# A hybrid HGRN2 and ConvFFN layer on one core: weights moved to byte 64 of their 256-byte lines, and products of 512 columns divided into two of 256

## The chip, the core and the metric

The kernel runs on one core of a Trainium2 chip. The core has a matrix engine (TensorE; its products stand in the profile as PE, its loads of the stationary operand as PEld), a vector engine (VectorE, DVE), a scalar engine (ScalarE, ACT), GpSimd (POOL) and a queue engine (SyncE, SP) that issues the transfers here. The metric is the device time of one execution in microseconds (us), as the median of several runs; lower is better.

## The reference

One layer of a diffusion backbone over 256 latent tokens and 256 context tokens of width 2048, in float32. It is cut here to what matters.

```python
h_l = modulate(rms_norm(x_lat, norm_mix_pre), sh_ml, sc_ml)      # shifts, scales, gates: silu(c) @ ada_w + ada_b
h_c = modulate(rms_norm(x_ctx, norm_mix_pre), sh_mc, sc_mc)
y_l, _ = hgrn2_mixer(h_l, h_c, w_in, lower_bounds, o_norm, w_out, False)   # w_in 2048 x 10240: q, f, b, v, g
x_lat = x_lat + gt_ml * rms_norm(y_l, norm_mix_post)             # w_out 2048 x 2048
h_l = modulate(rms_norm(x_lat, norm_ffn_pre), sh_fl, sc_fl)
gate, up = split(h_l @ ffn_w_in)                                 # 2048 x 11264
f_l = (silu(dwconv3(gate) ) * up) @ ffn_w_out                    # 5632 x 2048
return x_lat + gt_fl * rms_norm(f_l, norm_ffn_post)
```

The mixer is a gated linear recurrence in both directions over 16 heads of 128, in chunks. Its context half only makes the start state.

## The kernel before

**Products in three parts.** Every weight and every activation of the large products is split into two numbers in the format float32r: `split` (L95, L96) has ScalarE write the rounded `hi` and VectorE the rest `lo`. One product is then three of the matrix engine, in `mm3`: `hi*hi` (L192), `hi*lo` (L193) and `lo*hi` (L194), summed in one bank of PSUM. Each of the three loads its own stationary operand of 128 columns, also where it is the one loaded before.

**The weight stream.** `Stream` walks through 456 weight tiles of 512 KB each (128 partitions x 1024 numbers): 160 of `w_in`, 32 of `w_out`, 176 of `ffn_w_in`, 88 of `ffn_w_out`. Each is loaded into `w_raw` (4 buffers, line L117, queue SP), split by ScalarE into `w_hi` and by VectorE into `w_lo` (3 buffers each), and then used by the matrix engine. [...]

**Where operands lie.** The function `shifted` makes a buffer 32 numbers wider than the tile and puts tile number i of the stream 16*(i mod 8) bytes behind the buffer's start. A buffer is thus 4224 bytes wide, 16.5 times 256. In the built program the three `w_hi` buffers start at bytes 39424, 43648 and 47872 of each partition and the three `w_lo` buffers at 52096, 56320 and 60544: by their remainder to 256 at 0, 128, 0 and at 128, 0, 128. Together with the shift, a tile's `hi` lies at one of the 16 multiples of 16 below 256, and its `lo` always 128 away from it (modulo 256). The other operands have fixed remainders: the normed tokens of the mixer (`hTh`, `hTl`) and the FFN's inner activations (`ah`, `al`) 224, the mixer's output (`zh`, `zl`) 160, the tokens of the FFN's first product (`h2h`, `h2l`) 0. Slices of all these start whole multiples of 512 bytes further. Below, the offset of a product is the start of the stationary operand minus that of the moving one, modulo 256.

**Two directions, two widths.** In one direction weights are stationary and tokens move (the profile writes `pj<-hTh,w_hi`, moving operand first): 256 columns for q, g and for all of `ffn_w_in`, 512 columns for the f and b parts of `w_in` (latent and context tokens at once). In the other direction tokens are stationary and weights move (`pj<-w_hi,hTh`): 256 columns for v after the first two head pairs, 512 columns for v of these, for `w_out` (`pj<-w_hi,zh`) and for `ffn_w_out` (`pj<-w_hi,ah`).

**The order.** Five stages follow one another: the start (norms, the first parts of the modulation by `ada_w`, and four heads, all K at once), the other heads with the recurrence of earlier ones between the products (`scan`), the product with `w_out`, the FFN's first product, its second. Between them VectorE computes the other parts of the modulation from `ada_w` (`ada_part`, L344 and L346, tiles of 256 KB by the same queue SP, 3 buffers). A scheduler that knows shapes orders each engine's instructions within these bounds.

Of the kernel before, what the change touches and what calls it, by code (L numbers as in the profile page):

```python
# [8 lines left out]
F32 = mybir.dt.float32  # L9
F32R = mybir.dt.float32r  # L10
# [7 lines left out]
P = 128  # L18
# [17 lines left out]
def tile_hgrn2_convffn_layer(  # L36
# [17 lines left out]
    ps_mi = ctx.enter_context(tc.tile_pool(name="ps_mi", bufs=1, space=PSUM))  # L54
    ps_o = ctx.enter_context(tc.tile_pool(name="ps_o", bufs=1, space=PSUM))

    def bank(pool, name):
        return pool.tile([P, 512], F32, name=name)

# [35 lines left out]
        S.copy(out=hi, in_=src)  # L95
        V.tensor_tensor(out=lo, in0=src, in1=hi.bitcast(F32), op=ALU.subtract)  # L96

    def shifted(pool, a, w, name, i):

        t = pool.tile([P, a * w + 32], F32R, name=name)  # L100
        return t[:, 4 * i:4 * i + a * w].rearrange("p (a n) -> p a n", a=a)

    class Stream:


# [14 lines left out]
        def prep(self, pool=wpool):  # L120
            i = len(self.done)
            with tc.high_priority(offset=0 if i < n_start else 400):
                self.load(i + 1)
                _, a, w = self.specs[i]
                hi = shifted(pool, a, w, "w_hi", i % 8)
                lo = shifted(pool, a, w, "w_lo", i % 8)
                if i in self.fine:
                    for j in range(a):
                        split(hi[:, j], lo[:, j], self.raw[i][:, j])
                else:  # L130
                    split(hi, lo, self.raw[i])
            self.raw[i] = None
            self.done.append((hi, lo))
# [55 lines left out]

    def mm3(o, lhs, rhs, first, last):  # L190
        (lh, ll), (rh, rl) = lhs, rhs
        PE.matmul(out=o, lhsT=lh, rhs=rh, start=first, stop=False, skip_group_check=True)  # L192
        PE.matmul(out=o, lhsT=lh, rhs=rl, start=False, stop=False, skip_group_check=True)  # L193
        PE.matmul(out=o, lhsT=ll, rhs=rh, start=False, stop=last, skip_group_check=True)  # L194
# [311 lines left out]
    with tc.manual_schedule():  # L506
# [3 lines left out]
        nc.sync.dma_start(out=rowsB[0:96], in_=rows128(ada_b))  # L510
        nc.sync.dma_start(out=rows0[0:16], in_=rows128(n_mix_pre[0]))
        ws.load(1)
        aws0 = ada_load(0)
        ws.load(4)
        V.memset(ones32, 1.0)
# [386 lines left out]
    yp = y_ctx.enter_context(tc.tile_pool(name="yp", bufs=1, side="right"))  # L902
    zh = [yp.tile([P, 2, T], F32R, name=f"zh{p}") for p in range(NP)]
    zl = [yp.tile([P, 2, T], F32R, name=f"zl{p}") for p in range(NP)]
    h_ctx, xin_ctx = ExitStack(), ExitStack()
    h2h, h2l, xin, hold = [], [], [], []

    def mixed():

        nonlocal h2  # L910
        with tc.high_priority(offset=200):
            split(zh[1], zl[1], z[1])
        for p in (*range(2, NP - 1), 0):
            split(zh[p], zl[p], z[p])
            for _ in range(MIXSTEP):
                next(mix, None)
            yield
        for _ in mix:
            pass
        split(zh[NP - 1], zl[NP - 1], z[NP - 1])  # L920
        yield
        yield
        zp_ctx.close()
        sp_ctx.close()
        h2 = h_ctx.enter_context(tc.tile_pool(name="h2", bufs=1))
        for k in range(KT // 2):
            h2h.append(h2.tile([P, 2, T], F32R, name=f"h2h{k}"))
            h2l.append(h2.tile([P, 2, T], F32R, name=f"h2l{k}"))

        xinp = xin_ctx.enter_context(tc.tile_pool(name="xinp", bufs=1))  # L930
        hold.append(xin_ctx.enter_context(tc.tile_pool(name="hold", bufs=MORE)))
        for i in range(4):
            xin.append(xinp.tile([P, D // 2], F32, name=f"xin{i}"))
            nc.sync.dma_start(out=xin[i], in_=x[i // 2 * P:(i // 2 + 1) * P, i % 2 * 1024:(i % 2 + 1) * 1024])

    h2 = None
# [91 lines left out]
    for i in range(NFF):  # L1028
# [6 lines left out]
        for up in range(2):  # L1035
            o = bank(ps_pj, "pj")
# [72 lines left out]
```

## Time and profile before

| | us |
|---|---|
| median of 3 runs | 1764.19 (1764.08 to 1764.83) |
| the profiled execution | 1765.91 |
| its span | 1764.1 |
| matrix engine busy | 1718.5 (97%) |
| VectorE, ScalarE busy | 1158.9, 778.1 |
| mean granted clock of the matrix engine | 0.993 of full speed |

The profiled execution is 1.8 us longer than its span, and 1.7 us longer than the median. A matmul's busy time in the profile is its stay in the pipeline and overlaps with the next one's; how fast products follow one another is read from their starts, or from the number of products in a stretch that is busy throughout.

### The profile page before, as it was taken

The page shows a single profiled execution, that of the slowest core. Times are in us where ns is not written, and L with a number is a line of the kernel's source. Part 1 is how long each engine was busy: PE and PEld are TensorE (multiplying, and loading weights), DVE is VectorE, ACT ScalarE, POOL GpSimd, SP SyncE. Part 2 cuts the span into 40 slices and gives each one's busy share as a digit, 9 for nine tenths or more (in the row PEclk, how much of TensorE's full clock was granted, in tenths as well). Part 3 has the DMA queues.
Part 4 walks back from the last instruction along what each step waited for, and adds up shares of the span by engine and source line. Part 5 has one row for each costly group of instructions (what it writes and reads, how often), then busy time and mean ns, then how long its engine had stood idle before and what let it go on. Part 6 is the DMA issues. An engine that isn't in the chain of part 4 may idle for free.

```text
span 1764.1 us, 32106 instructions
## 1 busy us (share of the span) xinstructions
PE 1718.5 (97%) x13022; PEld 1530.1 (87%) x13022; DVE 1158.9 (66%) x1877; ACT 778.1 (44%) x1197; POOL 3.4 (0%) x13
## 2 busy tenths in 40 slices
PE   6999999999999999999999899999999999999998
PEld 4777788989889888988987699999999999888886
DVE  6777898855649775784667887565555565544444
ACT  4222264444545344443554644444444444443443
POOL 0000000000000000000000000000000000000000
PEclk9999999999999999999999899999999999999999
DMA  9887656643337764774368587566566565655554
GB/s 347 291 306 229 210 167 216 218 141 108 97 96 221 259 204 142 252 227 135 111 235 286 172 290 247 182 190 183 183 185 188 183 191 182 201 196 192 196 188 147
DMA packets 274646, 352.57 MB, mean 200 GB/s; under 512 B 12954, under 2 KB 197675, under 8 KB 273987
## 3 DMA queue, kind: packets, MB, share of 16 engines
q1 hardware_dynamic: 274499, 350.53, 61.6%
q8 instruction: 102, 1.67, 0.4%
q14 instruction: 45, 0.37, 0.1%
HBM read 348.37 MB, written 2.11 MB: 199 GB/s over the span
## 4 chain that ended last, share of the span: by engine, by line
PE 76%; DMA 11%; DVE 8%; issue 2%; ACT 2%; SPq 0%; DVEq 0%; ACTq 0%
PE pj L192 24%; PE pj L194 23%; PE pj L193 23%; DMA ada_w<-in_ada_w_dram 10%; DVE ada_acc L346 3%; DVE w_lo L96 2%; PE o L398 2%; PE sc L713 1%; ACT w_hi L95 1%; PE mi L785 1%; DMA aw<-in_ada_w_dram 0%; DVE k L673 0%; DMA w_raw<-in_hgrn_w_in_dram 0%; PE mi L701 0%; PE o L804 0%
## 5 line engine op out<-in xcount | busy, mean ns | idle before, releaser
L96 DVE TENSOR_TENSOR w_lo<-w_raw,w_hi 128x1024 fp32r<-128x1024 f32 (+1 forms) x465 | 558.5, 1203 | 383.8 <-ACT w_hi L95 382.6
L95 ACT CAST w_hi<-w_raw 128x1024 fp32r<-128x1024 f32 (+1 forms) x465 | 478.6, 1032 | 728.7 <-PE pj L193 395.7
L194 PE MATMUL pj<-h2h,w_lo 128*128 128x256 f32 x1408 | 395.9, 281 | 2.5 <-DVE w_lo L96 2.5
L193 PE MATMUL pj<-h2l,w_hi 128*128 128x256 f32 x1408 | 396.4, 282 | 0.1
L192 PE MATMUL pj<-h2h,w_hi 128*128 128x256 f32 x1408 | 396.0, 281 | 0.2 <-ACT h2h L95 0.2
L192 PE MATMUL pj<-hTh,w_hi 128*128 128x256 f32 (+1 forms) x1040 | 354.0, 341 | 2.8 <-ACT hTh L95 1.6
L194 PE MATMUL pj<-hTh,w_lo 128*128 128x256 f32 (+1 forms) x1040 | 347.9, 335 | 2.9 <-DVE w_lo L96 2.8
L193 PE MATMUL pj<-hTl,w_hi 128*128 128x256 f32 (+1 forms) x1040 | 348.0, 335 | 0.0
L194 PEld LDWEIGHTS pj<-h2h,w_lo 128*128 128x128 f32 x1408 | 265.8, 189 | 3.1 <-DVE w_lo L96 3.0
L192 PEld LDWEIGHTS pj<-h2h,w_hi 128*128 128x128 f32 x1408 | 265.7, 189 | 1.2 <-issue 0.8
L193 PEld LDWEIGHTS pj<-h2l,w_hi 128*128 128x128 f32 x1408 | 265.7, 189 | 0.3 <-DVE h2l L96 0.3
L346 DVE SCALAR_TENSOR_TENSOR ada_acc<-ada_w,cst,ada_acc 128x512 f32<-128x512 f32 x240 | 179.8, 749 | 77.9 <-DMA ada_w<-in_ada_w_dram 75.5
L192 PEld LDWEIGHTS pj<-hTh,w_hi 128*128 128x128 f32 x1040 | 195.5, 188 | 32.3 <-issue 5.9
L194 PEld LDWEIGHTS pj<-hTh,w_lo 128*128 128x128 f32 x1040 | 195.5, 188 | 25.7 <-DVE w_lo L96 3.5
L193 PEld LDWEIGHTS pj<-hTl,w_hi 128*128 128x128 f32 x1040 | 196.0, 188 | 21.0 <-DVE hTl L96 0.2
L192 PE MATMUL pj<-w_hi,ah 128*128 128x512 f32 x352 | 138.8, 394 | 0.0
L194 PE MATMUL pj<-w_hi,al 128*128 128x512 f32 x352 | 138.5, 393 | 0.0
L193 PE MATMUL pj<-w_lo,ah 128*128 128x512 f32 x352 | 138.1, 392 | 0.0
L192 PE MATMUL pj<-w_hi,hTh 128*128 128x256 f32 (+1 forms) x448 | 135.9, 303 | 1.3 <-DVE stage L448 0.7
L194 PE MATMUL pj<-w_hi,hTl 128*128 128x256 f32 (+1 forms) x448 | 133.8, 299 | 0.0
L193 PE MATMUL pj<-w_lo,hTh 128*128 128x256 f32 (+1 forms) x448 | 133.5, 298 | 0.0
L192 PEld LDWEIGHTS pj<-w_hi,hTh 128*128 128x128 f32 x448 | 85.0, 190 | 6.2 <-DVE stage L448 1.8
(224 smaller groups left out, 1778.8 us busy)
## 6 DMA issues: line engine op xcount, KB each, us to landing
w_raw<-in_ffn_w_in_dram SPq DMA_DIRECT2D x176, 512.0 KB, 4.5
w_raw<-in_hgrn_w_in_dram SPq DMA_DIRECT2D x160, 512.0 KB, 4.3
ada_w<-in_ada_w_dram SPq DMA_DIRECT2D x256, 256.0 KB, 3.9
w_raw<-in_ffn_w_out_dram SPq DMA_DIRECT2D x88, 512.0 KB, 3.7
aw<-in_ada_w_dram SPq DMA_DIRECT2D x64, 512.0 KB, 8.0
w_raw<-in_hgrn_w_out_dram SPq DMA_DIRECT2D x32, 512.0 KB, 5.6
hTh<-in_x_dram SPq DMA_DIRECT2D x2, 1024.0 KB, 7.1
hTh<-in_ctx_dram SPq DMA_DIRECT2D x2, 1024.0 KB, 11.8
```

Source lines behind the costliest of these rows:

```text
L95: S.copy(out=hi, in_=src)
L96: V.tensor_tensor(out=lo, in0=src, in1=hi.bitcast(F32), op=ALU.subtract)
L192: PE.matmul(out=o, lhsT=lh, rhs=rh, start=first, stop=False, skip_group_check=True)
L193: PE.matmul(out=o, lhsT=lh, rhs=rl, start=False, stop=False, skip_group_check=True)
L194: PE.matmul(out=o, lhsT=ll, rhs=rh, start=False, stop=last, skip_group_check=True)
L346: V.scalar_tensor_tensor(out=acc, in0=aw, scalar=cst[:, r, 0:1], in1=acc, op0=ALU.mult, op1=ALU.add)
L398: PE.matmul(out=strip[32 * a:32 * (a + 1), :], lhsT=cst[:, r4 * 4 + a, :], rhs=aws[r4][:, a].rearrange("p s n -> p (s n)"), start=(r4 == 0 ...
L713: PE.matmul(out=o[32 * b:32 * b + 32, 32 * i:32 * i + 32], lhsT=flat(lhs[b % 2])[:, s0:s0 + 32], rhs=flat(rhs[b % 2])[:, t0:t0 + 32], star ...
L785: PE.matmul(out=sps[:, cs], lhsT=kT[:, d, h, ct], rhs=v[:, 2 + ct, h * P:(h + 1) * P], start=(ct == 0), stop=(ct == 1))
```

## The change

Three things change. The buffers `w_hi` and `w_lo` lose the shift and are 4096 bytes wide; small unused tiles (`spacer`) are put into the pools so that every weight buffer starts 64 bytes behind a multiple of 256, and `hTh`, `hTl`, `h2h`, `h2l`, `zh`, `zl`, `ah` and `al` on a multiple of 256. In the built program this holds for all products but 24, those with the first split of head pair 0 (`z0`), where both operands are at 64. `hi` and `lo` of a tile thus have the same offset: 64 where weights are stationary, and minus 64, that is 192, where tokens are. And `mm3` divides a product of 512 moving columns into two of 256, each with its three parts.

```diff
+    def spacer(pool, nbytes):
+        pool.tile([P, nbytes // 4], F32, name="spacer", bufs=1)
+    SHIFT = 64
+    edge = ctx.enter_context(tc.tile_pool(name="edge", bufs=1, side="right"))
+    spacer(edge, 224)
...
-    def shifted(pool, a, w, name, i):
-        t = pool.tile([P, a * w + 32], F32R, name=name)
-        return t[:, 4 * i:4 * i + a * w].rearrange("p (a n) -> p a n", a=a)
...
-                hi = shifted(pool, a, w, "w_hi", i % 8)
-                lo = shifted(pool, a, w, "w_lo", i % 8)
+                hi = pool.tile([P, a, w], F32R, name="w_hi")
+                lo = pool.tile([P, a, w], F32R, name="w_lo")
...
     def mm3(o, lhs, rhs, first, last):
         (lh, ll), (rh, rl) = lhs, rhs
+        if rh.shape[-1] == 512:
+            for s in (slice(0, 256), slice(256, 512)):
+                mm3(o[:, s], lhs, (rh[:, s], rl[:, s]), first and s.start == 0, last and s.start > 0)
+            return
         PE.matmul(out=o, lhsT=lh, rhs=rh, start=first, stop=False, skip_group_check=True)
         PE.matmul(out=o, lhsT=lh, rhs=rl, start=False, stop=False, skip_group_check=True)
         PE.matmul(out=o, lhsT=ll, rhs=rh, start=False, stop=last, skip_group_check=True)
...
         ws.load(1)
+        spacer(wpool, SHIFT)
...
+    spacer(yp, 192)
...
         h2 = h_ctx.enter_context(tc.tile_pool(name="h2", bufs=1))
+        spacer(h2, 256 - SHIFT)
...
         hold.append(xin_ctx.enter_context(tc.tile_pool(name="hold", bufs=MORE)))
+        spacer(hold[0], SHIFT)
```

The built program grows from 11694 to 14814 products on the matrix engine: 3120 of 512 columns become 6240 of 256, each with a load of its stationary operand. 1488 of the 3120 (496 in each of the three parts) have stationary weights, 1632 stationary tokens.

On the matrix engine, where the FFN's second product begins, before (line, operation, output, moving and stationary operand with the tile's number, columns):

```order
L194 MATMUL pj<-h2h_10178,w_lo 128x256
L192 MATMUL pj<-w_hi,ah_10796 128x512
L193 MATMUL pj<-w_lo,ah_10796 128x512
L194 MATMUL pj<-w_hi,al_10797 128x512
L192 MATMUL pj<-w_hi,ah_10796 128x512
L193 MATMUL pj<-w_lo,ah_10796 128x512
L194 MATMUL pj<-w_hi,al_10797 128x512
```

And the same place after the change (lines are 10 further):

```order
L204 MATMUL pj<-h2h_11961,w_lo 128x256
L202 MATMUL pj<-w_hi,ah_12868 128x256
L203 MATMUL pj<-w_lo,ah_12868 128x256
L204 MATMUL pj<-w_hi,al_12869 128x256
L202 MATMUL pj<-w_hi,ah_12868 128x256
L203 MATMUL pj<-w_lo,ah_12868 128x256
L204 MATMUL pj<-w_hi,al_12869 128x256
L202 MATMUL pj<-w_hi,ah_12868 128x256
L203 MATMUL pj<-w_lo,ah_12868 128x256
L204 MATMUL pj<-w_hi,al_12869 128x256
L202 MATMUL pj<-w_hi,ah_12868 128x256
L203 MATMUL pj<-w_lo,ah_12868 128x256
```

Each group of three stands there twice, for the two halves of the columns.

On SP's queue, where the weights of the FFN's first product begin, before (`w_raw` is a weight tile, `ada_w` a tile of the modulation's last part):

```order
L117 DMA w_raw<-in_hgrn_w_out_dram 128x2x512
L342 DMA ada_w<-in_ada_w_dram 128x512
L117 DMA w_raw<-in_ffn_w_in_dram 128x4x256 x4
L342 DMA ada_w<-in_ada_w_dram 128x512 x3
L117 DMA w_raw<-in_ffn_w_in_dram 128x4x256 x3
L342 DMA ada_w<-in_ada_w_dram 128x512 x6
L117 DMA w_raw<-in_ffn_w_in_dram 128x4x256
L342 DMA ada_w<-in_ada_w_dram 128x512
```

And after the change:

```order
L122 DMA w_raw<-in_hgrn_w_out_dram 128x2x512
L352 DMA ada_w<-in_ada_w_dram 128x512
L122 DMA w_raw<-in_ffn_w_in_dram 128x4x256 x4
L352 DMA ada_w<-in_ada_w_dram 128x512 x4
L122 DMA w_raw<-in_ffn_w_in_dram 128x4x256 x3
L352 DMA ada_w<-in_ada_w_dram 128x512 x9
L122 DMA w_raw<-in_ffn_w_in_dram 128x4x256
L352 DMA ada_w<-in_ada_w_dram 128x512
```

Four more tiles of `ada_w` stand ahead of the ninth weight tile of the FFN. The loads, their number and their sizes are the same over the whole program; in the stage of the recurrence, too, some instructions of VectorE, ScalarE and SP stand a few places earlier or later than before.

## Rows read from the trace of the kernel before

**Rows 1.** The page: span, busy time by engine (share of the span, instructions).

```profile
span 1764.1 us, 32106 instructions
...
PE 1718.5 (97%) x13022; PEld 1530.1 (87%) x13022; DVE 1158.9 (66%) x1877; ACT 778.1 (44%) x1197; POOL 3.4 (0%) x13
```

**Rows 2.** Windows by stage: busy us (instructions), granted clock, DMA share, GB/s.

```profile
0.00:100.00 100.00, 82.41 (x554) 61.96 (x555) 67.43 (x142) 39.93 (x60) 1.38 (x9) 1.00 0.92 320
100.00:255.00 155.00, 155.00 (x859) 122.39 (x858) 125.71 (x226) 54.04 (x66) 0.00 (x0) 1.00 0.68 225
255.00:890.00 635.00, 627.89 (x5845) 561.34 (x5844) 443.74 (x887) 294.38 (x571) 0.99 (x2) 0.99 0.55 174
...
1005.00:1512.00 507.00, 504.21 (x4245) 502.46 (x4244) 322.17 (x382) 235.39 (x281) 0.53 (x1) 1.00 0.65 200
1512.00:1764.00 252.00, 244.74 (x1061) 198.47 (x1059) 118.07 (x109) 96.42 (x105) 0.00 (x0) 0.99 0.56 186
```

**Rows 3.** Groups by line and shape: count, busy us, mean ns of one.

```profile
L192 PE MATMUL pj<-h2h,w_hi 128*128 128x256 f32 x1408 | 396.0, 281 | 0.2 <-ACT h2h L95 0.2
...
L192 PE MATMUL pj<-hTh,w_hi 128*128 128x512 f32 x496 | 198.7, 401 | 0.0
...
L192 PE MATMUL pj<-hTh,w_hi 128*128 128x256 f32 x544 | 155.3, 287 | 2.8 <-ACT hTh L95 1.6 <-ACT w_hi L95 1.3
...
L192 PE MATMUL pj<-w_hi,ah 128*128 128x512 f32 x352 | 138.8, 394 | 0.0
...
L192 PE MATMUL pj<-w_hi,hTh 128*128 128x256 f32 x384 | 110.4, 287 | 0.0
```

**Rows 4.** Windows, matrix engine alone, inside the FFN's two products.

```profile
1250.00:1500.00 250.00, 250.00 (x2118) 1.00 0.61 186
1520.00:1740.00 220.00, 220.00 (x953) 1.00 0.58 193
```

**Rows 5.** Timeline, FFN's first product: first matmuls of weight tiles 51 to 54.

```profile
1156.79 0.28 PE L192 MATMUL pj<-h2h,w_hi 128*128 128x256 f32 x1
...
1159.63 0.28 PE L192 MATMUL pj<-h2h,w_hi 128*128 128x256 f32 x1
...
1162.36 0.28 PE L192 MATMUL pj<-h2h,w_hi 128*128 128x256 f32 x1
...
1165.19 0.28 PE L192 MATMUL pj<-h2h,w_hi 128*128 128x256 f32 x1
```

**Rows 6.** Timeline, the same product: first matmuls of tiles 60 and 61.

```profile
1182.27 0.28 PE L192 MATMUL pj<-h2h,w_hi 128*128 128x256 f32 x1
...
1185.13 0.28 PE L192 MATMUL pj<-h2h,w_hi 128*128 128x256 f32 x1
```

**Rows 7.** Timeline, mixer, 256 columns, stationary weights: one tile's first matmul, the next's.

```profile
733.31 0.28 PE L192 MATMUL pj<-hTh,w_hi 128*128 128x256 f32 x1
...
736.04 0.28 PE L192 MATMUL pj<-hTh,w_hi 128*128 128x256 f32 x1
```

**Rows 8.** Timeline, 512 columns, stationary weights: one tile's first matmul, the next's.

```profile
130.62 0.39 PE L192 MATMUL pj<-hTh,w_hi 128*128 128x512 f32 x1
...
136.19 0.40 PE L192 MATMUL pj<-hTh,w_hi 128*128 128x512 f32 x1
```

**Rows 9.** Timeline, 256 columns, stationary tokens: second and 47th matmul of one tile.

```profile
437.85 0.28 PE L193 MATMUL pj<-w_lo,hTh 128*128 128x256 f32 x1
...
443.16 0.28 PE L193 MATMUL pj<-w_lo,hTh 128*128 128x256 f32 x1
```

**Rows 10.** Windows over stretches with tiles of the modulation, columns as in rows 2.

```profile
550.00:650.00 100.00, 97.37 (x860) 87.37 (x847) 82.04 (x146) 42.90 (x80) 0.00 (x0) 1.00 0.76 245
...
900.00:1000.00 100.00, 90.83 (x389) 71.45 (x387) 68.31 (x100) 46.91 (x87) 0.53 (x1) 0.97 0.74 252
1000.00:1100.00 100.00, 95.59 (x777) 94.64 (x778) 82.30 (x122) 49.01 (x71) 0.00 (x0) 0.97 0.81 258
```

**Rows 11.** Longest waits of the matrix engine from 250 to 1100: us, times, longest.

```profile
PE pj L194 <- DVE w_lo L96: 5.1, 3, 2.6
```

## The prediction

> **What bounds the kernel now.** I read the page first: the matrix engine is busy for 97% of the span, VectorE for 66%, ScalarE for 44% [rows 1]. Then the windows by stage: from 100 us on the matrix engine is busy nearly throughout, and only in the first 100 us (82.4 of 100, transfers at a share of 0.92) does it wait for transfers [rows 2]. So what a product costs from one start to the next is the time of this kernel, apart from the start and from some waits that come later. The mean durations of the groups (281 ns for 256 columns, 394 ns for 512) overlap and are not that cost; I use these rows for the counts alone [rows 3].
>
> The cost comes from stretches that are busy throughout. Between 1250 and 1500 us there are 2118 products in 250 us, 118.0 ns each, all but a few with 256 columns and stationary weights. Between 1520 and 1740 us there are 953 in 220 us, 230.8 ns each, with 512 columns and stationary tokens [rows 4]. [...]
>
> [...] A weight tile of the FFN's first product is 24 products. Tile 52 takes from 1159.63 to 1162.36, that is 2.73 us or 113.75 ns a product; its neighbours 51 and 53 take 2.84 and 2.83 us, 118.3 and 117.9 ns [rows 5]. Nothing in the code differs between them but the addresses: tile 52 has `hi` at offset 64 and `lo` at 192, tile 51 has `hi` at 176, tile 53 at 80. Following the timeline through all 176 tiles, every undisturbed tile with `hi` at 64 takes 2.73 to 2.76 us, each time it comes round, and the other 15 offsets take 2.82 to 2.90. In the mixer, whose tokens lie at 224 instead of 0, a tile at relative offset 192 for `hi` and 64 for `lo` takes 2.73 us as well [rows 7]. In the FFN, however, tile 60, also 192 and 64, takes 2.86 us, 119.2 ns [rows 6]. So the offset matters and 64 is the good one for `hi`, with something beside it that I can't read off.
>
> **The change, part by part.**
>
> *Products of 256 columns with stationary weights.* There are 3 x 1408 of the FFN and 3 x 544 of the mixer [rows 3], 5856. The timeline of the first 100 us holds 240 of these, and there I count no gain since transfers set the pace: 5616 remain. All get offset 64, for `hi` and `lo`. No tile of before has both at 64. The price is bounded by tile 52 (113.75) and by tile 60 (119.2); I take 113.75, since tile 52 has two of its three loads at 64 and the mixer's tile shows that the third may be either. Gain 118.0 - 113.75 = 4.3 ns x 5616 = 24.1 us.
>
> *512 columns with stationary weights.* 3 x 496 = 1488 [rows 3], 48 of them before 100 us, so 1440. A tile with `hi` at offset 64 takes 5.57 us for 24, or 232.1 ns [rows 8]: at 512 columns the offset alone gives nothing visible. Two products of 256 at 113.75 are 227.5. Gain 4.6 ns x 1440 = 6.6 us. The halves bring a further load of the stationary operand each; it is in the 113.75, for a product of 256 has one too.
>
> *256 columns with stationary tokens.* 3 x 384 = 1152 [rows 3]. Their offset becomes 192 throughout. The nearest row is a tile with offsets 192, 64, 192 for its three parts: 45 products in 5.31 us, 118.0 ns [rows 9], no better than the average. The other end is 113.75, if one offset throughout does here what it does in the other direction. I take 116.6, two thirds of the way to the nearer row: gain 1.4 ns x 1152 = 1.6 us; ends 0 and 4.9.
>
> *512 columns with stationary tokens.* 3120 - 1488 = 1632, 55 of them before 100 us, so 1577, at 230.8 ns [rows 4]. Two of 256 at 116.6 are 233.2: a loss of 2.4 ns x 1577 = 3.8 us. Ends: 227.5 (gain 5.2 us) and 236.0 (loss 8.2 us).
>
> *What else is behind the matrix engine.* A faster matrix engine asks for weights sooner. In three stretches, 300 us together, tiles of the modulation share the queue, transfers are at 0.74 to 0.81, VectorE is busy for 68 to 82 of 100 us and the matrix engine for 91 to 97 [rows 10]; its longest wait there and in the mixer is for `lo` from VectorE (5.1 us in three pieces) [rows 11], and VectorE stands in its own order behind tiles of `ada_w` that it waits for. A part of the gain falls into such a wait: of 29 us over 1660 us, these 300 us hold 5.2; I take 3 back. The reordering of SP's queue (four more tiles of `ada_w`, 1 MB, ahead of the FFN's ninth weight tile) lies there too; at the 258 GB/s of that stretch [rows 10] it is 4 us of transfer, hidden as long as the four `w_raw` buffers are ahead, and up to 4 us where they are not. The other moves are within a few places and are counted at nothing; the busy matrix engine covers them. The longer program (6240 more instructions of the matrix engine's) I count at nothing as well: 2118 pairs of load and product follow one another in 250 us already, at the pace that the halves would need.
>
> *Sum.* -24.1 - 6.6 - 1.6 + 3.8 + 3 = -25.5 us. The profiled execution takes 1765.9 us, which gives 1740.4; its median of runs stands 1.7 lower, so **1739 us** (1764.2 - 25.5 = 1738.7).
>
> [...]
>
> **The rivals.**
>
> *Tokens gain too.* If offset 192 throughout serves the other direction as 64 does the first, all four prices are 113.75: -24.1 - 6.6 - 4.9 - 5.2 = -40.8, or **1725** with 2 taken back. For it: the offset is the same up to its sign, and the alternation by 128 between `hi` and `lo` is gone. Against: the tile of rows 9. Chance 0.27.
>
> *The offset gives nothing and dividing costs: slower.* One offset for `hi` and `lo` is new; tile 60 shows that the right offsets can still be slow. If 118.0 stays the price, the halves cost 236.0: 3.9 x 1440 + 5.2 x 1577 = 13.8 us, **1778**. It decides above a price of 116.4 ns with stationary weights, where (118.0 - 116.4) x (5616 + 2880) is 13.6 us and eats the gain. Against it: the good tile repeats at the same pace wherever it comes round. Chance 0.09.
>
> *Waits take the gain.* If the stretches with the modulation keep their length and the 1 MB moved ahead costs its 4 us, and tokens stay at 118.0: -24.1 - 6.6 + 8.2 + 5.2 + 4 = -13.3, **1751**. Chance 0.10.
>
> *The terms cancel* (for instance 115.5 with weights and 118.0 with tokens): 1764. Chance 0.04.
>
> **How the numbers follow.** The likeliest, with chance 0.5, is 1739. The range reaches to the case below, with a little for a price under 113.75, and above past the case of the waits: 1723 to 1755; outside are the slower case, the cancelling and what lies below. Within 0.2% (3.5 us), about what a measurement of this kernel can tell from no change, lies only the cancelling: faster 0.87, same 0.04, slower 0.09.
>
> **What would show it.** In the FFN's first product the same 250 us would hold 2190 to 2200 products instead of 2118, with every tile at 2.73 us and no tile slower than its neighbours; the stage would shrink from 507 to about 490 us. In the second product the 220 us would hold about 1887 halves (116.6 each); over 1906 of them and that stage has gained from being divided, under it has lost. The start's first 100 us would be unchanged, and the waits for `lo` between 900 and 1100 a little longer. I am wrong if tiles at one common offset run at 118 like the rest, if the price with stationary tokens is far from 116.6, or if waits grow by much more than 3 us.

## The result and the profile after

The changed kernel takes **1757.5 us** (median of 5; 1764.8 for the kernel before beside it). The ratio of the two is 0.9943 [0.9923, 0.9963], so it is 0.6% faster; the span of the profiled execution fell by 8.6 us, where 25.5 were forecast, and the time lies above the range. Executions more than 1.5% above a kernel's fastest are left out of the ratios here, though not of the medians: two of the changed kernel's five (1781.7 and 1786.4) and, of the experiments, one of e10's (1774.1), one of e12's (1765.9) and three of e7's four (1753 to 1754), so that e7 is read from its profiled execution alone. The profiled execution of the changed kernel took 1757.47 us, its span is 1755.5.

The page of the changed kernel, against [rows 1]:

```profile
span 1755.5 us, 38329 instructions
...
PE 1694.8 (97%) x16142; PEld 1645.1 (94%) x16142; DVE 1157.8 (66%) x1877; ACT 779.4 (44%) x1197; POOL 3.4 (0%) x13
```

Windows by stage of the changed kernel, against [rows 2] (columns as there; the scan ends at 897 instead of 886, the product with `w_out` at 1021 instead of 1005, the FFN's first product at 1508 instead of 1512):

```profile
0.00:100.00 100.00, 82.77 (x652) 67.89 (x653) 66.82 (x141) 39.70 (x60) 1.38 (x9) 0.98 0.93 312
256.00:897.00 641.00, 622.09 (x6897) 605.49 (x6885) 437.65 (x878) 291.20 (x565) 0.99 (x2) 0.98 0.54 170
897.00:1021.00 124.00, 110.11 (x881) 104.86 (x880) 89.84 (x149) 61.91 (x120) 1.05 (x2) 0.97 0.76 249
1021.00:1508.00 487.00, 484.38 (x4245) 482.98 (x4246) 317.30 (x374) 235.67 (x283) 0.00 (x0) 1.00 0.66 203
1508.00:1755.00 247.00, 239.43 (x2113) 239.24 (x2111) 117.95 (x108) 96.50 (x105) 0.00 (x0) 0.99 0.60 190
```

And the windows inside the FFN's two products, against [rows 4]:

```profile
1250.00:1500.00 250.00, 250.00 (x2209) 1.00 0.63 194
1520.00:1740.00 220.00, 220.00 (x1943) 1.00 0.61 192
```

The FFN's products hold what was forecast and more: 250 us hold 2209 products instead of 2118 (113.2 ns each), and 220 us hold 1943 halves instead of 953 wholes, also 113.2 ns, well over the 1906 from which dividing pays. The two stages are 26 us shorter. But the scan, whose products should have become cheaper too, takes 641.8 us instead of 630.4, and `w_out` 123.8 instead of 118.9 (from first to first product). In the scan's window the matrix engine idles 19 us of 641 (before 7 of 635).

What it waits for there, in the changed kernel from 250 to 1100 us, against [rows 11] (us, times, longest):

```profile
PE pj L204 <- DVE w_lo L106: 13.2, 5, 3.7
PE pj L203 <- DVE w_lo L106: 6.6, 8, 1.5
PE mi L365 <- DVE ada_acc L356: 5.3, 1, 5.3
```

So `lo` comes late from VectorE: the longest such group was 5.1 us in three pieces and is 13.2 in five. VectorE's timeline at two of these waits that follow each other (2.8 and 3.2 us; the longest, 3.7, comes later), changed kernel, weight tiles 107 to 110 of the stream (counted from 0):

```profile
617.91 1.21 DVE L106 TENSOR_TENSOR w_lo<-w_raw,w_hi 128x1024 fp32r<-128x1024 f32 x1
619.44 0.49 DVE L354 TENSOR_SCALAR ada_acc<-ada_w,cst 128x512 f32<-128x512 f32 x1 [0.31 <-DMA ada_w<-in_ada_w_dram]
620.17 1.54 DVE L356 SCALAR_TENSOR_TENSOR ada_acc<-ada_w,cst,ada_acc 128x512 f32<-128x512 f32 x2 [0.24 <-DMA ada_w<-in_ada_w_dram]
624.73 0.75 DVE L356 SCALAR_TENSOR_TENSOR ada_acc<-ada_w,cst,ada_acc 128x512 f32<-128x512 f32 x1 [3.02 <-DMA ada_w<-in_ada_w_dram]
625.39 1.22 DVE L106 TENSOR_TENSOR w_lo<-w_raw,w_hi 128x1024 fp32r<-128x1024 f32 x1
626.53 1.53 DVE L356 SCALAR_TENSOR_TENSOR ada_acc<-ada_w,cst,ada_acc 128x512 f32<-128x512 f32 x2
628.42 0.75 DVE L356 SCALAR_TENSOR_TENSOR ada_acc<-ada_w,cst,ada_acc 128x512 f32<-128x512 f32 x1 [0.36 <-DMA ada_w<-in_ada_w_dram]
632.13 0.75 DVE L356 SCALAR_TENSOR_TENSOR ada_acc<-ada_w,cst,ada_acc 128x512 f32<-128x512 f32 x1 [2.95 <-DMA ada_w<-in_ada_w_dram]
632.79 1.22 DVE L106 TENSOR_TENSOR w_lo<-w_raw,w_hi 128x1024 fp32r<-128x1024 f32 x1
633.93 1.53 DVE L356 SCALAR_TENSOR_TENSOR ada_acc<-ada_w,cst,ada_acc 128x512 f32<-128x512 f32 x2
635.62 0.75 DVE L356 SCALAR_TENSOR_TENSOR ada_acc<-ada_w,cst,ada_acc 128x512 f32<-128x512 f32 x1 [0.16 <-DMA ada_w<-in_ada_w_dram]
639.19 1.54 DVE L356 SCALAR_TENSOR_TENSOR ada_acc<-ada_w,cst,ada_acc 128x512 f32<-128x512 f32 x2 [2.82 <-DMA ada_w<-in_ada_w_dram]
640.65 1.22 DVE L106 TENSOR_TENSOR w_lo<-w_raw,w_hi 128x1024 fp32r<-128x1024 f32 x1
```

Read the order from top to bottom: between two `w_lo` stand four tiles of the modulation, four again, then five, and each time VectorE stands some 3 us before one whose transfer has not landed, with the `w_lo` behind it that the matrix engine waits for at the second and the third. What these two read was there long before: ScalarE (L105) had written their `w_hi` by 623.85 and 630.06 us, 8.9 and 10.6 us before VectorE began on them. The same place before, where groups of three, four and two tiles stand between these `w_lo`s and the matrix engine had one wait:

```profile
617.07 1.22 DVE L96 TENSOR_TENSOR w_lo<-w_raw,w_hi 128x1024 fp32r<-128x1024 f32 x1
618.20 2.38 DVE L346 SCALAR_TENSOR_TENSOR ada_acc<-ada_w,cst,ada_acc 128x512 f32<-128x512 f32 x3
620.50 1.22 DVE L96 TENSOR_TENSOR w_lo<-w_raw,w_hi 128x1024 fp32r<-128x1024 f32 x1
623.26 2.33 DVE L346 SCALAR_TENSOR_TENSOR ada_acc<-ada_w,cst,ada_acc 128x512 f32<-128x512 f32 x3 [1.54 <-DMA ada_w<-in_ada_w_dram]
628.00 0.75 DVE L346 SCALAR_TENSOR_TENSOR ada_acc<-ada_w,cst,ada_acc 128x512 f32<-128x512 f32 x1 [2.41 <-DMA ada_w<-in_ada_w_dram]
628.67 1.22 DVE L96 TENSOR_TENSOR w_lo<-w_raw,w_hi 128x1024 fp32r<-128x1024 f32 x1
629.80 1.53 DVE L346 SCALAR_TENSOR_TENSOR ada_acc<-ada_w,cst,ada_acc 128x512 f32<-128x512 f32 x2
631.25 1.22 DVE L96 TENSOR_TENSOR w_lo<-w_raw,w_hi 128x1024 fp32r<-128x1024 f32 x1
```

Slow products stand behind these two waits. Windows of the matrix engine alone there, changed kernel (busy, count, granted clock, transfers):

```profile
617.30:630.00 12.70, 12.70 (x115) 1.00 0.71 231
630.00:634.00 4.00, 1.26 (x12) 1.00 0.53 185
634.00:641.80 7.80, 4.61 (x24) 0.72 0.69 226
641.80:646.00 4.20, 4.08 (x19) 0.50 0.87 265
646.00:669.90 23.90, 23.84 (x338) 0.96 0.50 156
```

After the second wait 4.2 us hold 19 products at a granted clock of 0.50, where 37 of 113.3 ns would fit. So behind these two waits, of 2.8 and 3.2 us, the granted clock was 0.72 and 0.50, and each cost more than its length. The single wait of 2.6 us at this place before was not followed by a lower clock: from 626 to 634 us the granted clock is 1.00 throughout.

Below, the **excess** of a stretch is the sum of what the distance from a product's start to the start of the matrix engine's next instruction has above 118 ns (256 columns) or 232 ns (512), over all distances at least 30 ns longer than that. It holds waits and slow products. In the scan it is 18.2 us before and 39.2 after (of the 39, 21 are 20 distances of more than twice a product's price, so waits, and 18 are some 190 products at a little under twice their price). Each kernel has one profile, and kernels with the same order differ by some microseconds in it.

### The profile page after: what moved, and what is told of

The parts are those of the page before. It is cut to its first block, busy times and chain, and to the rows that moved or that the text cites. A ratio compares the mean times of both kernels' runs of the same rounds, so it can differ in the third digit from the quotient of the medians.

```text
span 1755.5 us, 38329 instructions
## 1 busy us (share of the span) xinstructions
PE 1694.8 (97%) x16142; PEld 1645.1 (94%) x16142; DVE 1157.8 (66%) x1877; ACT 779.4 (44%) x1197; POOL 3.4 (0%) x13
## 4 chain that ended last, share of the span: by engine, by line
PE 77%; DMA 11%; DVE 8%; issue 2%; ACT 2%; SPq 0%; DVEq 0%; ACTq 0%
PE pj L202 24%; PE pj L204 24%; PE pj L203 24%; DMA ada_w<-in_ada_w_dram 9%; DVE w_lo L106 2%; DVE ada_acc L356 2%; PE o L408 2%; PE sc L724 1%; ACT w_hi L105 1%; PE mi L796 1%; DMA w_raw<-in_hgrn_w_in_dram 1%; DVE k L684 1%; DMA aw<-in_ada_w_dram 1%; DMA w_raw<-in_hgrn_w_out_dram 0%; PE pj L336 0%
## 5 line engine op out<-in xcount | busy, mean ns | idle before, releaser
L105 ACT CAST w_hi<-w_raw 128x1024 fp32r<-128x1024 f32 (+1 forms) x465 | 478.6, 1032 | 723.9 <-PE pj L203 386.9
L204 PE MATMUL pj<-hTh,w_lo 128*128 128x256 f32 x1536 | 430.8, 281 | 11.4 <-DVE w_lo L106 11.3
L202 PE MATMUL pj<-hTh,w_hi 128*128 128x256 f32 x1536 | 436.7, 285 | 3.0 <-ACT hTh L105 1.6
L203 PE MATMUL pj<-hTl,w_hi 128*128 128x256 f32 x1536 | 430.5, 281 | 0.0
L203 PE MATMUL pj<-w_lo,ah 128*128 128x256 f32 x704 | 194.3, 276 | 0.0
L202 PE MATMUL pj<-w_hi,ah 128*128 128x256 f32 x704 | 194.3, 276 | 0.0
L204 PE MATMUL pj<-w_hi,al 128*128 128x256 f32 x704 | 194.3, 276 | 0.0
L202 PE MATMUL pj<-w_hi,hTh 128*128 128x256 f32 x512 | 145.0, 283 | 0.6 <-DVE q L460 0.6
L203 PE MATMUL pj<-w_lo,hTh 128*128 128x256 f32 x512 | 142.7, 279 | 0.0
L204 PE MATMUL pj<-w_hi,hTl 128*128 128x256 f32 x512 | 142.6, 279 | 0.0
L202 PEld LDWEIGHTS pj<-w_hi,ah 128*128 128x128 f32 x704 | 132.2, 188 | 0.0
```

## The experiments

Two theories stood against each other. **A:** dividing products makes the scheduler order VectorE's and SP's instructions differently, and that order makes the matrix engine wait. **B:** the faster matrix engine overtakes VectorE and the transfers, whatever the order. In this kernel the two parts of the change come apart cleanly: the new addresses alone leave every engine's order as it was, row for row; the division changes it.

**e1: new addresses, nothing divided.** In the changed kernel:

```diff
-        if rh.shape[-1] == 512:
-            for s in (slice(0, 256), slice(256, 512)):
-                mm3(o[:, s], lhs, (rh[:, s], rl[:, s]), first and s.start == 0, last and s.start > 0)
-            return
```

> The new addresses alone; products of 512 columns stay whole. The order of all engines is then that of the kernel before, row for row. Theory A (the new order of VectorE and SP, which comes with the divided products, makes the mixer wait): the stage of the recurrence has waits and half-clock products as before (about 14 us, not 40) and is shorter than before by its cheaper products of 256 columns (1152 x 4 ns + 1152 x 1 ns, 6 us); the FFN's first product is 21 us shorter as after the change, its second as before; in all about 1737 us. Theory B (a faster matrix engine overtakes VectorE and the transfers): the waits in that stage grow as after the change, it is no shorter than before, and the total is 1744 us or more.

Measured: 1744.6 us, ratio 0.9877 [0.9857, 0.9897]; scan 631.8, excess 25.0. By the signs set down, this lies between the two theories: the excess has taken on a third of what the changed kernel adds, but the total, and a scan no shorter than the 630.4 of before, are B's.

**e2: the division alone.** The same lines added to the kernel before, at the old addresses.

> The division alone, on the old addresses with their 16 offsets; the order of all engines is that of the changed kernel. Products of 256 columns should cost 118 ns as before, so two halves 236 in place of 231 to 232: 14 us more matmul time, 1778 us if nothing else changes. Theory A: the mixer's waits are there too, as after the change, about 25 us more than before, and the total is about 1800 us. Theory B: the matrix engine is not faster, so waits are as before or shorter, and the total is about 1778 us.

Measured: 1794.4 us, 1.0174 [1.0152, 1.0196]; scan 645.0, excess 31.9, `w_out` 124.1. Divided products come with waits even where none is faster than before, which B doesn't allow; the added excess is 13.7 us, where A expected some 25.

**e3: new addresses, `ffn_w_out` alone divided** (`mm3` gets an argument `halves` in place of the test for 512 columns, true only in the calls of the last product); order as before.

> New addresses, and only the products of ffn_w_out divided; order as before the change. The last stage should take 239 us (113.3 ns per half) instead of 244, everything else as with the addresses alone. Theory A: about 1732 us, faster than both kernels. Theory B: 1739 us or more.

Measured: 1742.0 us, 0.9864 [0.9841, 0.9886]; scan 630.6, excess 21.6, last product 239.5 us instead of 241.9 undivided. It beats both kernels, though by B's total (1739 or more), not by A's 1732; against e1 only the last product is clearly shorter, the totals' intervals overlap.

**e4: the splits asked for earlier.** In the changed kernel, since division doubles the instructions by which the distance is counted:

```diff
-            with tc.high_priority(offset=0 if i < n_start else 400):
+            with tc.high_priority(offset=0 if i < n_start else 800):
```

> The changed kernel with the distance by which a weight tile's split is put ahead in the scheduler doubled from 400 to 800 instructions, since a tile of divided products now has 48 products instead of 24. It changes order alone. Theory A: the waits for w_lo in the stage of the recurrence shrink by half or more and the total falls by 10 us or more, to about 1745 us. Theory B: little changes, about 1757 us.

Measured: 1756.5 us, 0.9958 [0.9938, 0.9977]; scan 636.9, excess 35.5. The repair failed. It doesn't speak against A: in the scan the tiles of the modulation stand on VectorE and SP at the same weight tiles as in the changed kernel, so the edit left in place the order that it was to change.

**e5 and e6: the division by place.** New addresses; e5 divides the f and b products alone, e6 those with `w_out` and `ffn_w_out`. In e5:

```diff
     def proj_ws(banks, wt, k4, width, first, last):
...
                 mm3(o, (hi[:, k, cs], lo[:, k, cs]), (hTh[kt][:, 0:width], hTl[kt][:, 0:width]),
-                    first and k == 0 and (own or h == 0), last and k == 3 and (own or h == 1))
+                    first and k == 0 and (own or h == 0), last and k == 3 and (own or h == 1), halves=width == 512)
```

> New addresses; of the products of 512 columns only those of the f and b parts of w_in are divided, w_out, ffn_w_out and the start's v are whole. VectorE's and SP's order differs from before only in the scan; from w_out on it is that of before. Theory A (the order that comes with the division makes the mixer wait): the scan takes 638 to 644 us as after the full change (641.8), w_out 115 to 118 and not 124, the FFN as with the offsets alone (490, 242): 1750 to 1755 us. Theory B (the faster matrix engine waits, order harmless): the halves' lower price is kept, the scan takes 626 to 630, and the whole 1737 to 1741.

> New addresses; only the products with w_out and ffn_w_out are divided. VectorE's and SP's order differs from before only from the product with w_out to the FFN's first product. Theory A: the scan stays at 630 to 632 us as with the offsets alone, w_out takes 122 to 125 (the matrix engine waits some 5 us for the modulation's sum), ffn_w_out 239.5: 1746 to 1751 us, 4 to 9 above the version with ffn_w_out alone divided (1742). Theory B: w_out 115 to 118, the whole 1740 to 1743.

Measured: e5 1750.1 us, 0.9924 [0.9906, 0.9942]; scan 638.0, excess 36.7, `w_out` 114.9. e6 1745.6 us, 0.9907 [0.9877, 0.9936]; scan 627.7, excess 19.8, `w_out` 121.6. Each loss comes where its own division is and not in the other stage, as A has it. All six profiles with `w_out` divided (the changed kernel, e2, e4, e6, e7, e9) have the matrix engine wait there for the sum of the modulation, 2.6 to 5.3 us, and none of the others has. In e6 the matrix engine's wait is the one of the changed kernel (e6, 884 to 1007 us):

```profile
PE mi L365 <- DVE ada_acc L356: 5.3, 1, 5.3
PE pj L203 <- DVE w_lo L106: 5.2, 5, 1.5
```

**e7 and e8: transfers of the modulation left out,** in the changed kernel and in the kernel before. Each part loads its first tile and uses it 64 times.

```diff
-                aw = pool.tile([P, 512], F32, name="ada_w", bufs=3)
-                nc.sync.dma_start(out=aw, in_=ada_w[...])
+                if b == 0 and r == 0:
+                    aw = pool.tile([P, 512], F32, name="ada_w", bufs=3)
+                    nc.sync.dma_start(out=aw, in_=ada_w[...])
```

> The changed kernel, in which each of the four later parts of the modulation loads only the first of its 64 tiles of ada_w and uses it 64 times: VectorE's and the matrix engine's work is the same, 252 transfers of 256 KB are left out and so the modulation's values are not the reference's. If VectorE standing behind tiles of ada_w that are late is what delays w_lo, the waits and the half clock of the scan go: their excess falls from 39 to under 12 us, the scan takes 610 to 617 instead of 641.8, w_out 115 to 119, the whole 1718 to 1728 us. If the order of VectorE's own work or the pace is the cause, without the transfers, the excess stays above 25 and the whole above 1740.

> The kernel before with the same 252 transfers left out, to stand beside the run on the changed kernel without them. The excess of its scan is 18 us, so no more than some 10 can go there and 5 at w_out: 1748 to 1756 us. With the waits out of both kernels the difference of the two is the matrix engine's alone: by the prices measured in the stages 35 us, by the prediction's four terms 28.5. If the difference is below 15, the prices are not kept for another reason than these transfers.

Measured: e7's profiled execution 1726.3 us, scan 620.7, excess 21.0; e8 1744.3, scan 622.1, excess 13.9. Of the 21 us that the change adds to the scan's excess (39.2 against 18.2) 7 are left without the transfers (21.0 against 13.9). The matrix engine's waits for `w_lo` go with them (0.3 us from 256 to 880 in e7, 11.3 in the changed kernel); others stay, so that the excess missed the 12 expected by A. e8 came out below its 1748 to 1756. The two kernels then differ by 18 us, between A's 28 to 35 and the 15 at which the prices would be in doubt; but that rests on one execution of e7, whose median of four is 1753.2. Nor are the orders kept: with the transfers left out, the modulation's instructions stand up to 10 (e7) and 9 (e8) weight tiles earlier on VectorE in the scan than before. So early a place made next to no wait for `w_lo` here, where no transfer had to land first.

**e9: the mixer's output moved by 256 bytes** (`spacer(yp, 448)` for `spacer(yp, 192)` in e6), because divided products of `w_out` take 117.8 ns and those of `ffn_w_out`, at the same offset modulo 256, 113.3.

> As the version with w_out and ffn_w_out divided, but the mixer's output zh, zl lies 256 bytes lower: offset 192 as before modulo 256, and modulo 512 now 192 (as for ffn_w_out, 113.3 ns) instead of 448 (117.8 ns with w_out). The order of every engine is the same. If the address modulo 512 sets the price, 744 halves of w_out go from 117.8 to 113.3 ns: 3.3 us, w_out's stage 118 instead of 121.6, the whole 1739 to 1743. If it is modulo 256, as the prediction assumed, nothing moves: 117.8 and 1742 to 1746.

Measured: 1746.0 us, 0.9904 [0.9872, 0.9935]; `w_out` still 117.8 ns. The address modulo 512 is not the reason; what is stays open.

**e10: small products as breaks.** In e3's FFN:

```diff
                 if 0 < i:
                     next(ada, None)
+                if i % 2 and k4 == 0 and not up:
+                    PE.matmul(out=bank(ps_o, "o")[:, 0:32], lhsT=ident, rhs=ident[:, 0:32], start=True, stop=True)
```

> As the version with ffn_w_out alone divided, with one small product of 32 columns put ahead of the gate part's first tile in every second of the FFN's 22 steps (11 in all, their result unused). In the runs so far tiles at one address run at 113.3 or at 117.8 ns a product for long stretches and change over only at a tile with a wait in it. If such a break is what changes the pace, it changes at these 11 places or at waits and nowhere else, in one direction or the other, and the stage comes out between 479 and 500 us: 1735 to 1755. If the address alone sets the pace, all tiles stay at 113.3 after the first twenty, and the breaks cost 11 times some 0.2 us: 1742 to 1746.

Measured: 1748.9 us, 0.9897 [0.9845, 0.995]. The edit didn't do what it was meant to: nothing ties the small products to a tile, and the engine ran all of them in one heap, ahead of the FFN (two records each):

```profile
L1056 PE MATMUL o<-ident x22: 195/276/401, 991.3 to 998.0; 128*128 128x32 f32 x22
```

Columns: shortest, median and longest in ns, first and last start in us. What breaks do at will is thus untried. But the profile caught a change of pace all the same: tiles 16 to 23 of the FFN's first product run at 117.8 ns, and at tile 24 the pace becomes 113.3, with no wait of another engine's making. First products of tiles 23 to 26, and two around a distance of 144 ns (1081.51 to 1081.65):

```profile
1078.44 0.28 PE L202 MATMUL pj<-h2h,w_hi 128*128 128x256 f32 x1
...
1081.27 0.28 PE L202 MATMUL pj<-h2h,w_hi 128*128 128x256 f32 x1
...
1081.51 0.31 PE L204 MATMUL pj<-h2h,w_lo 128*128 128x256 f32 x1
1081.65 0.28 PE L202 MATMUL pj<-h2h,w_hi 128*128 128x256 f32 x1
...
1084.05 0.28 PE L202 MATMUL pj<-h2h,w_hi 128*128 128x256 f32 x1
...
1086.77 0.28 PE L202 MATMUL pj<-h2h,w_hi 128*128 128x256 f32 x1
```

24 products take 2.83 us, then 2.78, then 2.72.

**e11: weights 192 bytes behind** (`SHIFT = 192` in e3; stationary weights at 192, stationary tokens at 64).

> As the version with ffn_w_out alone divided, but weights lie 192 bytes behind a multiple of 256 instead of 64: stationary weights have offset 192 and stationary tokens 64, the two swapped. The order is the same. If the price is good at 64 alone for stationary weights, as the prediction read it from tile 52, the FFN's first product goes back to 118 ns: 4224 times 4.5, 19 us, the whole 1760 or more. If 64 and 192 are alike in both directions, every stage keeps its length: 1739 to 1745.

Measured: 1754.7 us, 0.9942 [0.9922, 0.9962]. The FFN's first product is back at 117.8 ns in every tile (507.5 us; 250 us hold 2125), the last one keeps 113.3, the scan is 6 us shorter than e3's (624.9).

**e12: the modulation spread** (`ADA_RATE = 2.4`, and `if p >= 2` for `if p >= 3`, in e3).

> The version with ffn_w_out alone divided, with the modulation's tiles spread over more of the scan: begun one head pair earlier (from pair 2), at 2.4 tiles a step instead of 3. If tiles of ada_w that come late at VectorE are what makes the waits and the half clock in the scan (excess 21.5 us there), fewer of them a step leaves less: excess 8 to 15, the scan 617 to 625, the whole 1728 to 1737. If the order or the pace is the cause rather than the crowding of these transfers, the excess stays at 20 or above and the whole at 1740 to 1745.

Measured: 1740.1 us, 0.9845 [0.9811, 0.988]; scan 628.1, excess 23.9. Fewer tiles a step don't lower the excess; it moved (below). Since the edit also puts the modulation's tiles up to 14 weight tiles earlier on VectorE, it doesn't tell crowding and order apart.

By then one question was open: the division itself, or the order that comes with it? The order differs only in parts of the scan. Put down by weight tile, the excess of the profiled executions so far is (us; a head pair has 20 tiles, the scan begins with pair 2 at tile 40; "shifted": where with all f and b divided tiles of the modulation stand 1 to 4 weight tiles earlier on VectorE and SP):

| weight tiles | 43–62, shifted | 63–83 | 84–105 | 106–114, shifted | 115–126 | 127–145, shifted |
|---|---|---|---|---|---|---|
| before | 6.0 | 2.2 | 2.1 | 3.4 | 0.9 | 2.0 |
| e1 | 6.7 | 2.2 | 2.2 | 6.9 | 0.9 | 4.6 |
| e3 | 5.3 | 2.2 | 2.1 | 7.3 | 0.9 | 2.4 |
| e6 | 5.0 | 2.2 | 2.1 | 6.1 | 0.9 | 1.9 |
| e5 | 7.2 | 2.2 | 4.1 | 11.0 | 1.1 | 9.6 |
| changed kernel | 9.9 | 2.2 | 6.0 | 11.3 | 1.1 | 7.2 |
| e7 | 7.3 | 2.2 | 5.9 | 0.6 | 1.1 | 2.3 |
| e12 | 5.1 | 2.4 | 5.9 | 0.6 | 1.1 | 7.1 |

In e1, e3, e6 and e12 no product of the scan is divided, in e5, e7 and the changed kernel all of f and b are (the first eight tiles of each pair: 40 to 47, 60 to 67 and so on). Columns two and five hold 16 divided tiles (63 to 67, 80 to 83, 120 to 126) with the old order, and their excess is what it was, 2.2 and about 1. But, e12 apart, VectorE has no tile of the modulation at tiles 63 to 91 and 115 to 124, so this shows only that division makes no waits where little or no modulation runs beside it.

What tells more is where the added excess stands. At tiles 48 to 59, 108 to 114 and 128 to 139 (q, v and g) all products have 256 columns, so they are divided in no kernel. Their excess is 9.7 us before and 26.7 in the changed kernel: 17 of the 21 us that the change adds. The eight profiles at the new addresses with the old order in the scan and all transfers (e1, e3, e6, e9, e10, e11, e13, e15) have 10.7 to 16.9 there; the four with all f and b divided and all transfers (changed kernel, e2, e4, e5) have 22.6 to 26.7.

**e13 and e14: one head pair or two divided.** In e3, of the f and b products those of pairs 3 and 4 alone (order nearly that of before), or those of pair 5 alone (order shifted from tile 106 on):

```diff
-                    first and k == 0 and (own or h == 0), last and k == 3 and (own or h == 1))
+                    first and k == 0 and (own or h == 0), last and k == 3 and (own or h == 1),
+                    halves=width == 512 and pair[0] in (5,))
```

> New addresses, ffn_w_out divided, and of the f and b products those of head pairs 3 and 4 alone (weight tiles 60 to 67 and 80 to 87). SP's and the matrix engine's order is that of before, VectorE's differs in a few rows. If the order of the modulation's tiles makes the waits, none are added: excess in the scan 20 to 24 us as with f and b whole (21.5), the whole 1739 to 1745. If divided products make them by themselves, a third of the 14 us comes, most of it at tiles 60 to 105 (2.8 us with f and b whole, 7 with all divided): 1744 to 1749.

> New addresses, ffn_w_out divided, and of the f and b products those of head pair 5 alone (weight tiles 100 to 107). With it the modulation's tiles stand 1 to 3 weight tiles earlier on VectorE and SP at weight tiles 106 to 118, and nowhere else. If that order makes the waits, the excess at tiles 106 to 114 rises from 5 to 7 us to 10 to 11 as with all f and b divided, and elsewhere stays (43 to 62: 5 to 7; 127 to 145: 1.4 to 4.2): the whole 1743 to 1748. If the order is harmless, 5 to 7 there: 1739 to 1744.

Measured: e13 1740.2 us, 0.9853 [0.9829, 0.9878]; excess 20.7, at tiles 63 to 105 4.3 as in e3. e14 1744.4 us, 0.9884 [0.9856, 0.9913]; tiles 106 to 114 have 9.5, a little short of the 10 expected (3.3 to 7.3 in nine profiles with the old order there), the scan 27.8. Its tiles 43 to 62 have 8.0 where 5 to 7 were expected and nothing differs from e3: one or two microseconds in a column are scatter. Waits of the matrix engine for `w_lo` in the scan of e13, and of e14 (256 to 890 us):

```profile
PE pj L204 <- DVE w_lo L106: 3.0, 2, 2.1
```

```profile
PE pj L204 <- DVE w_lo L106: 6.1, 3, 4.4
```

The sixteen divided tiles of e13 add no wait, but 13 of them stand where no modulation runs beside them; the eight of pair 5, with tiles of the modulation moved ahead, add some behind them. With the excess at tiles that no kernel divides, and with e2, where nothing is faster, it is the new order that makes most of the waits, not the division of the products that wait. A kernel with the changed order and no divided product was not run.

**e15: 192 for the mixer, 64 for the FFN** (e3 with `SHIFT = 192` and `spacer(h2, 192)`, so that `h2h` lies 128 behind).

> As the version with ffn_w_out alone divided (weights 64 behind in both stages: scan 630.6, FFN's first product 491.1), but weights lie 192 bytes behind the mixer's operands and 64 behind the FFN's tokens. The order is the same. If the good address belongs to the width and the stage, the mixer keeps the 625 us it had with 192 and the FFN's first product the 487 to 491 it had with 64: 1733 to 1739, the fastest version. If the mixer's 625 was chance, the scan takes 630 and the whole 1740 to 1744.

Measured: 1748.5 us, 0.9897 [0.9874, 0.9921]. The scan takes 625.0 again and the FFN's first product 487.9, as expected, but the last product takes 248.9 us, where e11 with stationary tokens at the same 64 has 239.5. Windows inside the last product of e11 and, below it, of e15:

```profile
1510.00:1730.00 220.00, 220.00 (x1944) 1.00 0.62 198
```

```profile
1490.00:1710.00 220.00, 220.00 (x1870) 1.00 0.61 191
```

113.2 ns and 117.6 ns for the same products at the same offset and clock, with no wait in either. So one address had two paces here.

## Why the prediction was wrong

**The price of a product was right in sum, in part by luck.** Worked out from the starts, all distances without excess summed, the stages changed by -0.9 us (start), -9.6 (scan), +1.6 (`w_out`), -18.3 (FFN's first product) and -4.8 (its second): -32.0 against -28.5 for the four terms. The largest term, 4.3 ns for 256 columns with stationary weights, is met to a tenth in the FFN's first product (4224 times 4.3 are 18.2). The luck: at the same address e4 and e9 run through most of its first 78 tiles at 117.8 ns, next to no gain, and the changed kernel through its first 17. Stationary tokens were mis-sized: 113.3 ns in `ffn_w_out` instead of 116.6, a gain of 4.8 us instead of a loss of 2.5 there; in `w_out`, at the same offset, 117.8 instead of 116.6. So neither the tile of [rows 9] with its mixed offsets nor one common offset told the price. Half of the 4.8 us comes without dividing: undivided at the new addresses, the last product takes 241.9 us (e1) instead of 244.4, and the prediction counted whole products of 512 columns at one price whatever their offset. "Tokens gain too" was half right.

**The step that failed is the cover:** "The other moves are within a few places and are counted at nothing; the busy matrix engine covers them", and with it the 3 us taken back for all waits. The span fell by 8.6 us, the products by 32.0; 23.4 went elsewhere: 21.0 to the scan, 3.3 to `w_out`, where the matrix engine now waits 5.3 us for the sum of the modulation, and the rest nearly cancels. The runs divide the scan's part: with the new addresses and the order of before there (e1, e3, e6, e9, e10, e11, e15) its excess is 18.8 to 25.0, 21.7 in the mean, 3.5 above before; with f and b divided and the order that comes of it (e5 and the changed kernel) 36.7 and 39.2. So the pace took back some 3.5 us, about the 3 that were forecast for it (a rough figure, since before has one profile and the seven scatter over 6 us), and the order some 16 more in the scan. In `w_out` it took some 5: the stage has 122 to 124 us (123.3 in the mean) in four profiles in which it is divided at the new addresses and 114 to 119 (116.0) in nine in which it isn't, and 2.4 of the difference are the price. The prediction looked at SP's 1 MB ahead of the FFN, which cost nothing visible (the FFN's first stage met its 490 us), and not at the moves of one to four weight tiles on VectorE in the scan. There are three buffers of `w_lo` to cover a late one, and VectorE already stood behind the modulation's transfers before (256 to 900 us):

```profile
DVE ada_acc L346 <- DMA ada_w<-in_ada_w_dram: 49.9, 47, 3.3
```

The prediction named these waits, but as a reason why a faster pace would lose 3 us, and not as one why each place in VectorE's order counts.

**The rivals.** "Waits take the gain" (1751) had the right kind of cause and the wrong place and size: tokens did not stay at 118 in the last product, the 1 MB cost nothing, and the waits were mostly of the order's making. "The offset gives nothing" is out: the halves alone are 1.7% slower (e2), the addresses alone 1.2% faster (e1). "The terms cancel" is out with e1 as well.

**What stays open.** Without the transfers the added excess at tiles 106 to 145 goes almost wholly (e7: 0.6 and 2.3), but at tiles 43 to 62 and 84 to 105 it is 7.3 and 5.9, against 3.1 and 4.0 in e8; what makes it there was not separated. At tiles 84 to 105 the modulation's tiles stand where they stood, yet the excess is 1 to 4 us higher when all f and b are divided. Part of it is another wait: at tile 104 the matrix engine waits 1.7 us for `tmp` of the recurrence from ScalarE (609.3 us, changed kernel; 2.4 in e7, none before), and slow products follow it. And why two paces exist at one address was not found.

## What to carry to other kernels

A change of the matrix engine's instructions alone can reorder every other engine's queue where a scheduler lays them out; try the two parts of such a change apart, and divide products only where nothing else is left to be ordered (here the last product: 1742 us, with pairs 3 and 4 as well 1740, against 1757 with all; 1742 and 1740 are within each other's intervals). Where an engine stands in its order before transfers that have not landed (VectorE here, some 3 us at a time), count each place that such a waiting instruction moves ahead of one that the bound engine needs. Read the price of a product from one address throughout, and from several stretches, since the same product ran at two paces here (113.3 and 117.8 ns).

## What the runs showed of the hardware

**Two paces at one address.** With stationary weights at offset 64 a product of 256 columns took either 113.3 or 117.8 ns, tile after tile. In e4 the FFN's first product ran at 117.8 for most of its first 79 tiles and at 113.3 from there. Its windows on both sides:

```profile
1070.00:1220.00 150.00, 150.00 (x1276) 1.00 0.62 190
1300.00:1450.00 150.00, 150.00 (x1326) 1.00 0.64 195
```

150 us hold 1276 products or 1326 at the same addresses and a granted clock of 1.00. The pace changed over, in either direction, at a distance between two products that was longer than the rest: a wait of microseconds, but also the 144 ns in e10, and in e5 one of 124 ns, after which the slower pace began (tile 22 of the FFN's first product). At offset 192, stationary weights kept to 117.8 in all undisturbed tiles of e11's FFN; stationary tokens had 113.3 at 192 in all ten profiles with `ffn_w_out` divided there, and at 64 had either (e11, e15), but in `w_out`, at 192 too, 117.8 in all five profiles that divide it at the new addresses. So in the FFN's first product the faster pace with stationary weights was had at 64 (113.3 in e4) and not at 192 (117.8 in e11), and it began or ended at such a longer distance; what makes the pace change was not found, nor what decides for tokens. The two paces of the last product are 9.4 us apart, about the scatter of e15's executions (1743 to 1752). They are not shown to be its cause: the one profiled, with the slower pace in the last product, is the second shortest of the six.

**In the scan the better address differed by width.** There, undisturbed products of 512 columns with stationary weights start every 233.3 ns at offset 64 (e3) and every 229.1 at 192 (e11), before 232.3 at mixed offsets; those of 256 columns every 113.8 and 116.7, before 117.9. Stationary tokens there take 116.5 (e3) and 114.3 (e11). e15 has e11's figures to a tenth. That is how the scan is shorter at 192 although its products of 256 columns with stationary weights are slower.

**No 24 products of 256 columns in a row went below 113.3 ns each,** from start to start, in the profiles of the kernel before (113.5 at the least) and of the changed one (113.3).
